# Values of the cross attention from 512 weight columns per matmul, in a three-mixer decoder trunk on one core

## The chip, the core and the metric

The program runs on one core of a Trainium2 chip. It is launched once, and the metric is the device time of that launch in microseconds (us). Names of engines are those of the profile: PE multiplies matrices (PEld are its weight loads), ACT, DVE and POOL work element by element, SP starts most transfers from device memory. A program is written as one stream; a scheduler orders the instructions of each engine and puts semaphores between them, and each engine then works its own list in that order.

## What is computed

Four layers on 256 tokens of width 1024, float32. A layer is a token mixer (Mamba-2, HGRN2, gated DeltaNet, then Mamba-2 again), a cross attention into 256 memory tokens, and a gated feed-forward block. The part that the change touches is the product of the normalised memory with the second half of `wkv`, once per layer:

```python
def memory_cross_attention(h, mem_n, wq, wkv, wo):
    q = (h @ wq).reshape(bsz, seq, X_HEADS, X_HEAD_DIM)
    k, v = jnp.split(mem_n @ wkv, 2, axis=-1)
    ...
    s = jnp.einsum('blhd,bmhd->bhlm', q, k).astype(jnp.float32) * X_HEAD_DIM ** -0.5
    p = jax.nn.softmax(s, axis=-1).astype(h.dtype)
    o = jnp.einsum('bhlm,bmhd->blhd', p, v).reshape(bsz, seq, D_MODEL)
    return o @ wo
```

Here `mem_n` is 256 x 1024 and each half of `wkv` 1024 x 1024.

## The kernel before

Every product with weights is made of three matmuls. A float32 number is split into a rounded part H and a rest L, both in the type fp32r, and `mm3` (lines 166 to 170) adds H·H, H·L and L·H into one bank of PSUM. The memory is split once per layer into `mH` and `mL` (`mem_split`), while the feed-forward block of the layer before is running. The weights are split as they arrive: `prep` (lines 150 to 164) fetches a piece of 128 x 1024 numbers (512 KB) through SP's queue into the tile `raw`, rounds it on ACT (`wH`, line 160) and subtracts on DVE (`wL`, line 161). There are four buffers of `raw`, three of `wH` and three of `wL`, shared by all products with weights in the program. `prep` runs under a raised priority (300), so the scheduler places its instructions as far ahead of the matmuls as the buffers allow.

`mem_kv` (lines 344 to 383) makes keys and values of a layer ahead of its mixer. Its first half is the keys, its second half the values. For each of four blocks of 256 output columns it takes two pieces (`kh`, 512 rows of the weights each) and issues 48 matmuls in groups of three:

```python
                            if half == 0:
                                c = slice(k * T + cb * P, k * T + (cb + 1) * P)
                                mm3(d, H[:, c], L[:, c], mH[:, kt, :], mL[:, kt, :], first, last)
                            else:
                                c = slice(k * T, (k + 1) * T)
                                t = slice(cb * P, (cb + 1) * P)
                                mm3(d, mH[:, kt, t], mL[:, kt, t], H[:, c], L[:, c], first, last)
```

For the values the memory is the operand that is loaded into the array (128 columns of it), and 256 columns of a weight piece stream past it. So the values of one layer are 4 x 2 x 2 x 4 x 3 = 192 matmuls of 256 columns, into four banks named `kvps`. ACT then moves a bank to the tile `Vt`, scaled (line 353). DVE moves the keys to `KTt` (line 349).

What stands around this in a layer from the second on: the last products of the feed-forward block (`f_down`, in `out_proj`, banks `acc`), whose last four pieces are half as large; then DVE adds the banks to the residual `xT` (line 283), ACT squares it (`nsq`, line 200), POOL sums the squares (`ns`, lines 203 and 206), and a matmul `ps_nrm` (line 210) in the middle of the keys sums over partitions. From its result the normalised input of the mixer is made (`nh`, `hH`, `hL`) while PE is at the keys. After the values PE goes on with the mixer's first product, in the bank `fps` (HGRN2), `baps` (gated DeltaNet) or `dtps` (Mamba-2). Small latency-bound parts of the program are woven in between by a counter of estimated PE time (`weave.tick`). The first layer makes the sums of squares of the memory along with its keys (`stats` is not None there), at a time when the first transfers of the program are running.

Pools opened by `phase` take SBUF one behind the other and are given back when they close; a tile in a new pool waits for the instructions that used the same addresses before.

Of the kernel before, what the change touches and what calls it, by code (L numbers as in the profile page):

```python
# [8 lines left out]
F32 = mybir.dt.float32  # L9
F32R = mybir.dt.float32r  # L10
U32 = mybir.dt.uint32
AF = mybir.ActivationFunctionType
ALU = mybir.AluOpType
# [3 lines left out]
P = 128  # L17
D = 1024
T = 256
KT = 8  # L20
# [3 lines left out]
PRIO = 400  # L24
# [62 lines left out]
def tile_trunk(ctx: ExitStack, tc: tile.TileContext, io: dict, out: bass.AP, layers=range(DEPTH), parts="mxf", final=True):  # L87
    nc = tc.nc
    ACT, DVE, POOL, PE = nc.scalar, nc.vector, nc.gpsimd, nc.tensor
    weave = Weave()  # L90
# [7 lines left out]
    PRIO, EVAC = [300,150]  # L98
# [9 lines left out]
    def phase(name, bufs=1):  # L108
        return tc.tile_pool(name=name, bufs=bufs, reuse_waits="tile")
# [4 lines left out]
    def bank(name):  # L114
        return ps_acc.tile([P, 512], F32, tag="acc", name=name)
# [8 lines left out]
    def f32(ap):  # L124
        return ap.bitcast(F32)
# [10 lines left out]
    Vt = cst.tile([P, 2, D], F32, name="Vt")  # L136
# [10 lines left out]
    rsmc = cst.tile([P, 2], F32, name="rsmc")  # L147
# [4 lines left out]
    def prep(src, n=1024, step=1024):  # L152
        with tc.high_priority(offset=PRIO):
            raw = wp.tile([P, 1024], F32, tag="raw", name="raw", bufs=WB[0])
            H = wp.tile([P, 1024], F32R, tag="wH", name="wH", bufs=WB[1])
            L = wp.tile([P, 1024], F32R, tag="wL", name="wL", bufs=WB[2])
            for o in range(0, n, step):
                c = slice(o, min(n, o + step))
                nc.sync.dma_start(out=raw[:, c], in_=src[:, c])
                ACT.copy(H[:, c], raw[:, c])  # L160
                DVE.tensor_tensor(out=L[:, c], in0=raw[:, c], in1=f32(H[:, c]), op=ALU.subtract)  # L161
                if len(between) > 1:
                    between[-1](between.pop(0))
        return H, L

    def mm3(dst, aH, aL, bH, bL, start, stop):

        PE.matmul(dst, aH, bH, start=start, stop=False, skip_group_check=True)  # L168
        PE.matmul(dst, aH, bL, start=False, stop=False, skip_group_check=True)  # L169
        PE.matmul(dst, aL, bH, start=False, stop=stop, skip_group_check=True)  # L170
# [58 lines left out]
    def proj(srcs, ps):  # L229

        for i, s in enumerate(srcs):
            H, L = prep(s)
            for kt in range(KT):
                c = slice(kt * P, (kt + 1) * P)
                mm3(ps[:, i * T:(i + 1) * T], H[:, c], L[:, c], hH[:, kt, :], hL[:, kt, :],
                    i == 0 and kt == 0, kt == KT - 1)
                if kt % 2:
                    weave.tick(654)

    def proj_tok(srcs, ps):  # L240

        for kh, s in enumerate(srcs):
            H, L = prep(s)
            for mt in range(2):
                for k in range(4):
                    kt = 4 * kh + k
                    t = slice(mt * P, (mt + 1) * P)
                    c = slice(k * T, (k + 1) * T)
                    mm3(ps[:, mt * T:(mt + 1) * T], hH[:, kt, t], hL[:, kt, t], H[:, c], L[:, c],
                        kt == 0 and mt == 0, kt == KT - 1)  # L250
                    if k % 2:
                        weave.tick(654)

    def out_proj(wsrc, nk, a, gens=None, gname=None, layer=0, last=False):
# [5 lines left out]
        for g in range(ng):  # L260
# [10 lines left out]
            for b in range(4):  # L271
                H, L = prep(wsrc[g, b], n * T)
                for cb in range(2):
                    for k in range(n):
                        kt = 4 * g + k
                        c = slice(k * T + cb * P, k * T + (cb + 1) * P)
                        mm3(accs[b][:, cb * T:(cb + 1) * T], H[:, c], L[:, c], aH[k], aL[k],
                            kt == 0 and cb == 0, kt == nk - 1)
                        if k % 2:
                            weave.tick(654)  # L280
                if g == ng - 1:
                    xs = flat(xT[:, 2 * b:2 * b + 2, :])
                    DVE.tensor_tensor(out=xs, in0=xs, in1=accs[b], op=ALU.add)
                    if gname is not None:
                        for kt in (2 * b, 2 * b + 1):
                            split_gain(xT[:, kt, :], pcol(gname, layer * 8 + kt), hH[:, kt, :], hL[:, kt, :])
                    st.add(xs)
                    if last:
                        for kt in (2 * b, 2 * b + 1):
                            fg = pcol("final", kt)  # L290
                            if b < 3:
                                POOL.tensor_scalar(out=KTt[:, kt, :], in0=xT[:, kt, :], scalar1=fg, scalar2=None, op0=ALU.mult)
                            else:
                                ACT.activation(out=KTt[:, kt, :], in_=xT[:, kt, :], func=AF.Copy, scale=fg)
# [42 lines left out]
    def mem_rs(stats):  # L337
        stats.rs(rsm)
        tp = mx("rsmt")
        for mt in range(2):  # L340
            PE.transpose(tp[:, mt * P:(mt + 1) * P], rsm[:, mt * P:(mt + 1) * P], ident)
        ACT.copy(rsmc, tp[:, :T].rearrange("p (a b) -> p a b", a=2)[:, :, 0])

    def mem_kv(layer, mH, mL, stats=None):
        todo = []

        def evac(half, b, ps):
            if half == 0:
                DVE.tensor_tensor(out=KTt[:, 2 * b:2 * b + 2, :], in0=ps.rearrange("p (a b) -> p a b", a=2),
                                  in1=rsm.unsqueeze(1).to_broadcast([P, 2, T]), op=ALU.mult)  # L350
            else:
                for mt in range(2):
                    ACT.activation(out=Vt[:, mt, b * T:(b + 1) * T], in_=ps[:, mt * T:(mt + 1) * T], func=AF.Copy,
                                   scale=rsmc[:, mt:mt + 1])

        for half in range(2):
            for b in range(4):
                ps = bank("kvps")
                for kh in range(2):
                    H, L = prep(io["xa_kv"][layer, half, b, kh], step=512 if stats is not None else 1024)  # L360
                    for cb in range(2):
                        for k in range(4):
                            kt = 4 * kh + k
                            d = ps[:, cb * T:(cb + 1) * T]
                            first, last = kt == 0 and cb == 0, kt == KT - 1
# [7 lines that stand above are left out]
                            if k % 2:  # L373
                                weave.tick(654)
                todo.append((half, b, ps))
                if stats is not None:
                    if b == 0:
                        continue
                    mem_rs(stats)
                    stats = None  # L380
                for u in todo:
                    evac(*u)
                todo = []


    def attention(layer, st):
# [773 lines left out]
    for i, l in enumerate(layers):  # L1160
        nrm = weave.push(late(NL[0], norm_h(st, "ln_mix", l) if i else x_stats())) if mix else None
        if m is not None:
            mem_kv(l, *m)
            kv.close()
        if mix:
            weave.finish([nrm])
            st = (mamba, hgrn, gdn)[l % 3](l, l // 3, "ln_xattn" if "x" in parts else "ln_ffn" if "f" in parts else None)
        else:
            for kt in range(KT):
                g = "ln_xattn" if "x" in parts else "ln_ffn"  # L1170
                split_gain(xT[:, kt, :], pcol(g, l * 8 + kt), hH[:, kt, :], hL[:, kt, :])
        if "x" in parts:
            st = attention(l, st)
        m, hook = mem_start(i + 1)
        if "f" in parts:
            st = ffn(l, st, hook, final and i == len(layers) - 1)
        elif hook is not None:
            hook()
# [5 lines left out]
    for b in range(4):  # L1184
        o = Vt.rearrange("p a (b t) -> p (a b) t", t=T)[:, 2 * b:2 * b + 2, :]
        (POOL if b == 3 else DVE).tensor_tensor(out=o, in0=KTt[:, 2 * b:2 * b + 2, :],
                                                in1=rs.unsqueeze(1).to_broadcast([P, 2, T]), op=ALU.mult)
# [123 lines left out]
```

## Time and profile before

| | us |
|---|---|
| median of 3 runs | 2069.55 |
| the three runs | 2066.68, 2069.55, 2073.19 |
| the profiled execution | 2072.47 |
| its span, from its first to its last instruction | 2070.7 |
| PE busy in the span | 2025.5 (98%) |
| DVE busy | 1590.6 (77%) |
| ACT busy | 1282.5 (62%) |
| POOL busy | 344.5 (17%) |

The profile shows one execution. A matmul's busy time overlaps that of the next one, since matmuls are pipelined: what a matmul costs in a stream is read from the distance between starts, not from its own length. The profile's span and the time of the execution differ by 1.8 us that lie around the program.

### The profile page before, as it was taken

To read this page: it belongs to the slowest core of one execution; us is meant where nothing else is said; L and a number is where in the kernel's file an instruction comes from. 1 tells how busy PE (TensorE), PEld (TensorE's weight loads), DVE (VectorE), ACT (ScalarE), POOL (GpSimd) and SP (SyncE) were. 2 spreads that over 40 slices of the span, in tenths; PEclk is the share of its full clock that TensorE was granted. 3 is DMA by queue.
4 is the path that set the end of the run, shared out by engine and by line. 5 is a ranking of instruction groups with operands and counts; after the bars stand their busy time and mean duration, and the time that the engine had idled before them with its cause. 6 is when DMAs were issued, how large, how long until landed. Compare 5 with 4: busy or idle time off the path is not lost.

```text
span 2070.7 us, 42162 instructions
## 1 busy us (share of the span) xinstructions
PE 2025.5 (98%) x17084; PEld 1971.5 (95%) x17084; DVE 1590.6 (77%) x2423; ACT 1282.5 (62%) x1874; POOL 344.5 (17%) x468
## 2 busy tenths in 40 slices
PE   8999999999999999999999999999999999999997
PEld 8999999999999899999988889999999999999997
DVE  6899787875688777866786775778757999778765
ACT  6677666654565566555676875666545777666553
POOL 2032211000132110001064451110000223201001
PEclk9999999999999999999999999999999999999999
DMA  7554555655654446666543333456656444545663
GB/s 239 163 155 152 162 154 162 206 188 170 206 157 140 149 137 195 203 195 192 186 130 126 114 113 115 139 163 211 195 179 196 151 154 150 174 133 183 186 189 115
DMA packets 110372, 343.10 MB, mean 166 GB/s; under 512 B 15456, under 2 KB 25312, under 8 KB 110176
## 3 DMA queue, kind: packets, MB, share of 16 engines
q1 hardware_dynamic: 106176, 333.42, 52.0%
q10 hardware_dynamic: 3744, 6.71, 1.0%
q8 instruction: 134, 2.20, 0.4%
q0 software_dynamic: 256, 0.26, 0.1%
q14 instruction: 62, 0.51, 0.1%
HBM read 336.42 MB, written 3.93 MB: 164 GB/s over the span
## 4 chain that ended last, share of the span: by engine, by line
PE 79%; DVE 6%; issue 5%; ACT 4%; DMA 3%; POOL 2%; ACTq 0%; SPq 0%; DVEq 0%; POOLq 0%
PE acc L168 7%; PE ffps L170 7%; PE acc L169 7%; PE ffps L169 7%; PE ffps L168 7%; PE acc L170 7%; PE mps L168 4%; PE mps L169 4%; PE mps L170 4%; DVE wL L161 2%; PE kvps L170 2%; PE kvps L168 2%; PE kvps L169 2%; PE qps L170 2%; PE qps L168 2%
## 5 line engine op out<-in xcount | busy, mean ns | idle before, releaser
L161 DVE TENSOR_TENSOR wL<-raw,wH 128x1024 fp32r<-128x1024 f32 (+2 forms) x639 | 776.1, 1216 | 318.9 <-ACT wH L160 316.6
L160 ACT CAST wH<-raw 128x1024 fp32r<-128x1024 f32 (+2 forms) x639 | 658.4, 1031 | 510.6 <-PE ffps L169 156.4
L168 PE MATMUL acc<-aH,wH 128*128 128x256 f32 x1408 | 396.4, 282 | 0.6 <-ACT aH L173 0.6
L170 PE MATMUL ffps<-hH,wL 128*128 128x256 f32 x1408 | 392.6, 279 | 1.8 <-DVE wL L161 1.7
L168 PE MATMUL ffps<-hH,wH 128*128 128x256 f32 x1408 | 392.0, 279 | 2.5 <-ACT hH L183 2.5
L170 PE MATMUL acc<-aH,wL 128*128 128x256 f32 x1408 | 393.0, 279 | 0.0
L169 PE MATMUL acc<-aL,wH 128*128 128x256 f32 x1408 | 392.4, 279 | 0.1
L169 PE MATMUL ffps<-hL,wH 128*128 128x256 f32 x1408 | 392.1, 279 | 0.2
L168 PEld LDWEIGHTS ffps<-hH,wH 128*128 128x128 f32 x1408 | 265.5, 189 | 3.4 <-ACT hH L183 3.3
L168 PEld LDWEIGHTS acc<-aH,wH 128*128 128x128 f32 x1408 | 265.2, 189 | 3.5 <-issue 1.3
L170 PEld LDWEIGHTS ffps<-hH,wL 128*128 128x128 f32 x1408 | 264.4, 188 | 4.1 <-DVE wL L161 3.7
L169 PEld LDWEIGHTS acc<-aL,wH 128*128 128x128 f32 x1408 | 265.6, 189 | 1.5 <-issue 0.5
L169 PEld LDWEIGHTS ffps<-hL,wH 128*128 128x128 f32 x1408 | 265.1, 188 | 1.1 <-DVE hL L184 0.6
L170 PEld LDWEIGHTS acc<-aH,wL 128*128 128x128 f32 x1408 | 264.6, 188 | 0.4 <-DVE wL L161 0.2
L168 PE MATMUL mps<-hH,wH 128*128 128x256 f32 x768 | 219.8, 286 | 0.0
L170 PE MATMUL mps<-hH,wL 128*128 128x256 f32 x768 | 215.0, 280 | 0.0
L169 PE MATMUL mps<-hL,wH 128*128 128x256 f32 x768 | 214.9, 280 | 0.0
L203 POOL TENSOR_TENSOR ns<-nsq 128x256 f32<-128x256 f32 x13 | 10.5, 811 | 856.5 <-ACT nsq L200 856.5
L168 PEld LDWEIGHTS mps<-hH,wH 128*128 128x128 f32 x768 | 145.1, 189 | 2.7 <-issue 2.4
L170 PEld LDWEIGHTS mps<-hH,wL 128*128 128x128 f32 x768 | 145.4, 189 | 0.1
L169 PEld LDWEIGHTS mps<-hL,wH 128*128 128x128 f32 x768 | 144.5, 188 | 0.3
L170 PE MATMUL gps<-hH,wL 128*128 128x256 f32 x448 | 127.2, 284 | 0.9 <-DVE wL L161 0.9
(397 smaller groups left out, 4489.9 us busy)
## 6 DMA issues: line engine op xcount, KB each, us to landing
raw<-f_up SPq DMA_DIRECT2D x176, 512.0 KB, 3.6
raw<-m_in SPq DMA_DIRECT2D x96, 512.0 KB, 3.5
raw<-f_down SPq DMA_DIRECT2D x80, 512.0 KB, 3.5
raw<-xa_kv SPq DMA_DIRECT2D x60, 512.0 KB, 4.2
raw<-g_in SPq DMA_DIRECT2D x48, 512.0 KB, 3.9
raw<-m_out SPq DMA_DIRECT2D x32, 512.0 KB, 3.5
raw<-xa_q SPq DMA_DIRECT2D x32, 512.0 KB, 3.5
raw<-xa_o SPq DMA_DIRECT2D x32, 512.0 KB, 3.5
```

The costliest lines, as they stand in the source:

```text
L160: ACT.copy(H[:, c], raw[:, c])
L161: DVE.tensor_tensor(out=L[:, c], in0=raw[:, c], in1=f32(H[:, c]), op=ALU.subtract)
L168: PE.matmul(dst, aH, bH, start=start, stop=False, skip_group_check=True)
L169: PE.matmul(dst, aH, bL, start=False, stop=False, skip_group_check=True)
L170: PE.matmul(dst, aL, bH, start=False, stop=stop, skip_group_check=True)
L203: self.eng.tensor_tensor(out=self.sum, in0=sq[:, :T], in1=sq[:, T:], op=ALU.add)
```

## The change

From the second layer on the values are made by a new function, `wide_values`. Two blocks of 256 columns are taken together: `prep2` fetches a pair of pieces, rounds and subtracts each as `prep` does, but into tiles of their own (`raw2`, `wH2`, `wL2`) in a pool that exists for the values alone. Each matmul streams 512 columns, 256 from each piece of the pair, into a whole bank `vps`. A layer's values are 96 matmuls of 512 columns and four instructions on ACT that move 512 columns each to `Vt`. The raised priority of `prep2` is a third of `prep`'s, and there are two buffers of each of its tiles, for four pairs. The first layer keeps the old form. Keys are unchanged.

```diff
+    def prep2(srcs, pool):
+
+        with tc.high_priority(offset=PRIO // 3):
+            raw = pool.tile([P, 2, 1024], F32, tag="raw2", name="raw2")
+            H = pool.tile([P, 2, 1024], F32R, tag="wH2", name="wH2")
+            L = pool.tile([P, 2, 1024], F32R, tag="wL2", name="wL2")
+            for i in range(2):
+                nc.sync.dma_start(out=raw[:, i, :], in_=srcs[i])
+                ACT.copy(H[:, i, :], raw[:, i, :])
+                DVE.tensor_tensor(out=L[:, i, :], in0=raw[:, i, :], in1=f32(H[:, i, :]), op=ALU.subtract)
         return H, L
...
+    def wide_values(layer, mH, mL):
+
+        with phase(f"vw{layer}", 2) as vw:
+            vw.tile([P, 48], F32, name="vpad", bufs=1)
+            for b in range(2):
+                pv = [bank("vps") for _ in range(2)]
+                for kh in range(2):
+                    H, L = prep2([io["xa_kv"][layer, 1, 2 * b + i, kh] for i in range(2)], vw)
+                    for mt in range(2):
+                        t = slice(mt * P, (mt + 1) * P)
+                        for k in range(4):
+                            kt = 4 * kh + k
+                            c = slice(k * T, (k + 1) * T)
+                            mm3(pv[mt], mH[:, kt, t], mL[:, kt, t], H[:, :, c], L[:, :, c], kt == 0, kt == KT - 1)
+                            weave.tick(600)
+                for mt in range(2):
+                    ACT.activation(out=Vt[:, mt, b * 512:(b + 1) * 512], in_=pv[mt], func=AF.Copy,
+                                   scale=rsmc[:, mt:mt + 1])
+
     def mem_kv(layer, mH, mL, stats=None):
         todo = []
+        wide = stats is None
...
-        for half in range(2):
+        for half in range(1 if wide else 2):
...
+        if wide:
+            wide_values(layer, mH, mL)
```

The change also moves the splitting of the pairs in the lists of the engines. On DVE, at the end of the first layer's feed-forward block, the list before reads as follows (`wL_6537` and `wL_6560` belong to the last two half pieces of `f_down`, `wL_6585` to the first piece of the keys):

```order
L161 TENSOR_TENSOR wL_6537<-raw_6535,wH_6536 128x512
L283 TENSOR_TENSOR xT_79<-xT_79,acc0_5841 128x512
L161 TENSOR_TENSOR wL_6560<-raw_6558,wH_6559 128x512
L283 TENSOR_TENSOR xT_79<-xT_79,acc1_5842 128x512
L161 TENSOR_TENSOR wL_6585<-raw_6583,wH_6584 128x1024
L283 TENSOR_TENSOR xT_79<-xT_79,acc2_5843 128x512
L161 TENSOR_TENSOR wL_6615<-raw_6613,wH_6614 128x1024
```

With the change DVE's list at the same place is this; the first half of pair 2 stands first, its second half comes between the last half piece of `f_down` and the first piece of the keys:

```order
L175 TENSOR_TENSOR wL2_6908<-raw2_6906,wH2_6907 128x1024
L161 TENSOR_TENSOR wL_6514<-raw_6512,wH_6513 128x512
L161 TENSOR_TENSOR wL_6537<-raw_6535,wH_6536 128x512
L295 TENSOR_TENSOR xT_79<-xT_79,acc0_5841 128x512
L161 TENSOR_TENSOR wL_6560<-raw_6558,wH_6559 128x512
L175 TENSOR_TENSOR wL2_6908<-raw2_6906,wH2_6907 128x1024
L161 TENSOR_TENSOR wL_6585<-raw_6583,wH_6584 128x1024
L295 TENSOR_TENSOR xT_79<-xT_79,acc1_5842 128x512
```

Pairs 1 and 2 are thus split ahead of the keys, and the addition to the residual from the second bank has moved behind the first piece of the keys. The same holds in the two later layers.

On ACT, at the values of the second layer, the list before is:

```order
L160 CAST wH_6962<-raw_6961 128x1024
L160 CAST wH_6995<-raw_6994 128x1024
L353 ACTIVATE Vt_81<-kvps_6867,rsmc_94 128x256 x2
L160 CAST wH_7025<-raw_7024 128x1024
L160 CAST wH_7058<-raw_7057 128x1024
L353 ACTIVATE Vt_81<-kvps_6930,rsmc_94 128x256 x2
```

With the change ACT's list there is this (`wH_7137` is the third piece of the mixer that follows; `wH2_6944` is pair 3, `wH2_6977` pair 4):

```order
L160 CAST wH_7137<-raw_7136 128x1024
L174 CAST wH2_6944<-raw2_6943 128x1024 x2
L372 ACTIVATE Vt_81<-vps_6871,rsmc_94 128x512
L174 CAST wH2_6977<-raw2_6976 128x1024 x2
L372 ACTIVATE Vt_81<-vps_6872,rsmc_94 128x512
L372 ACTIVATE Vt_81<-vps_6941,rsmc_94 128x512
L372 ACTIVATE Vt_81<-vps_6942,rsmc_94 128x512
L680 DMA hc_7017<-cm 128x388
```

Three pieces of the mixer now stand ahead of pairs 3 and 4, which are the only weights split during the values.

## Rows read from the trace of the kernel before

**Rows 1.** The page: busy time, share of the span and instructions, and the chain's shares.
```profile
PE 2025.5 (98%) x17084; PEld 1971.5 (95%) x17084; DVE 1590.6 (77%) x2423; ACT 1282.5 (62%) x1874; POOL 344.5 (17%) x468
...
PE 79%; DVE 6%; issue 5%; ACT 4%; DMA 3%; POOL 2%; ACTq 0%; SPq 0%; DVEq 0%; POOLq 0%
```

**Rows 2.** Windows: two f_down stages, then the three values stages that change.
```profile
core 0: us, PE busy (x) PEld busy (x) DVE busy (x) ACT busy (x) POOL busy (x), PEclk, DMA share, GB/s
...
892.94:952.78 59.84, 59.84 (x530) 59.84 (x529) 34.10 (x38) 30.45 (x36) 1.59 (x2) 1.00 0.61 180
458.42:520.61 62.19, 62.19 (x531) 62.19 (x529) 34.23 (x37) 30.51 (x36) 1.72 (x2) 1.00 0.56 172
543.66:566.27 22.61, 22.61 (x195) 22.61 (x194) 11.04 (x12) 10.61 (x14) 0.00 (x0) 1.00 0.65 194
975.00:996.76 21.76, 21.76 (x194) 21.76 (x193) 10.78 (x12) 10.09 (x14) 0.00 (x0) 1.00 0.63 193
1572.32:1594.08 21.76, 21.76 (x194) 21.76 (x193) 10.85 (x13) 9.99 (x14) 0.00 (x0) 1.00 0.60 191
```

**Rows 3.** Groups by line on PE in the values stage from 975.00 (one of three).
```profile
L168 PE MATMUL kvps<-wH,mH 128*128 128x256 f32 x64 | 17.7, 276 | 0.0
```

**Rows 4.** Timeline of PE: end of values, layer two; first mixer product, layer four.
```profile
566.15 0.28 PE L170 MATMUL kvps<-wH,mL 128*128 128x256 f32 x1
566.27 0.28 PE L168 MATMUL fps<-hH,wH 128*128 128x256 f32 x1
...
1594.08 0.28 PE L168 MATMUL dtps<-hH,wH 128*32 128x256 f32 x1
...
1596.83 0.28 PE L168 MATMUL mps<-hH,wH 128*128 128x256 f32 x1
```

**Rows 5.** Instructions of two tiles: weight loads, ns min/median/max, first and last start.
```profile
L168 PEld LDWEIGHTS kvps<-wH,mH x256: 187/187/188, 33.7 to 1593.6; 128*128 128x128 f32 x128
...
L168 PEld LDWEIGHTS dtps<-hH,wH x16: 107/108/108, 56.5 to 1596.4; 128*32 128x32 f32 x16
```

**Rows 6.** Timeline of PE around one wait in the first layer's f_up.
```profile
392.80 0.28 PE L168 MATMUL ffps<-hH,wH 128*128 128x256 f32 x1
...
395.52 0.28 PE L168 MATMUL ffps<-hH,wH 128*128 128x256 f32 x1
...
396.37 0.39 PE L170 MATMUL ffps<-hH,wL 128*128 128x256 f32 x1 [0.45 <-DVE wL L161]
396.59 0.28 PE L168 MATMUL ffps<-hH,wH 128*128 128x256 f32 x1
...
400.12 0.28 PE L168 MATMUL ffps<-hH,wH 128*128 128x256 f32 x1
```

**Rows 7.** Timeline of ACT and DVE in the values stage from 975.00.
```profile
980.64 1.06 ACT L160 CAST wH<-raw 128x1024 fp32r<-128x1024 f32 x1 [1.62 <-PE kvps L170]
981.60 0.82 ACT L353 ACTIVATE Vt<-kvps,rsmc 128x256 f32<-128x256 f32 x2
...
981.73 1.23 DVE L161 TENSOR_TENSOR wL<-raw,wH 128x1024 fp32r<-128x1024 f32 x1 [1.45 <-ACT wH L160]
```

**Rows 8.** The page, DMA issues: KB each, median us to landing.
```profile
raw<-xa_kv SPq DMA_DIRECT2D x60, 512.0 KB, 4.2
```

**Rows 9.** Timeline of ACT, DVE, PE where f_down gives way to the keys, layer three.
```profile
950.22 1.04 ACT L160 CAST wH<-raw 128x1024 fp32r<-128x1024 f32 x1
...
950.26 0.69 DVE L283 TENSOR_TENSOR xT<-xT,acc 128x512 f32<-128x512 f32 x1
951.30 1.23 DVE L161 TENSOR_TENSOR wL<-raw,wH 128x1024 fp32r<-128x1024 f32 x1 [0.35 <-ACT wH L160]
...
952.78 0.28 PE L168 MATMUL kvps<-mH,wH 128*128 128x256 f32 x1
```

**Rows 10.** Timeline of POOL and PE: sums of squares and the matmul that takes them.
```profile
951.93 7.91 POOL L206 TENSOR_TENSOR ns<-ns,nsq 128x256 f32<-128x256 f32 x6 [0.79 <-ACT nsq L200]
...
963.66 0.38 PE L210 MATMUL ps_nrm<-ns,ones 128*128 128x256 f32 x1
```

More of the change, by code (lines that the diff above doesn't have):

```diff
@@ L163, in prep @@
                     between[-1](between.pop(0))
+        return H, L
+    def prep2(srcs, pool):
[7 more added lines that the diff above has]
+                DVE.tensor_tensor(out=L[:, i, :], in0=raw[:, i, :], in1=f32(H[:, i, :]), op=ALU.subtract)
         return H, L
```

## The prediction, made before the changed kernel was run

> **What bounds the kernel now.** I read the page first: PE is busy 98% of the span and holds 79% of the chain that ended last, while DVE stands at 77% and ACT at 62% [rows 1]. So time is won where PE needs fewer nanoseconds, and lost where PE is made to wait. Second, the windows over the three values stages that change: 22.61, 21.76 and 21.76 us, in each of which PE is busy from end to end, at a granted clock of 1.00, with ACT busy about 10 us and DVE about 11 [rows 2]. The groups by line show 64 matmuls of 256 columns for each of the three products [rows 3], 192 in all. The last of them and the first of the mixer start 0.12 us apart, like any two neighbours [rows 4]: there is no wait at that end which a faster stage could run into or remove.
>
> Third, the pace. 21.76 us over 192 is 113.3 ns from start to start, 22.61 over 192 is 117.8 ns. The two f_down stages, 528 equal matmuls each (22 x 4 x 2 x 3), give 59.84/528 = 113.3 and 62.19/528 = 117.8 [rows 2]. So PE has two paces, 4% apart, at the same granted clock, and each holds for whole stages. In the first layer's f_up I see one turn into the other: 24 matmuls in 2.72 us (113.3) up to 395.52, a wait for a subtraction at 396.37, then 30 in 3.53 us (117.7) [rows 6]. I don't know what sets the pace; a wait of PE can change it.
>
> At the granted level of 2.4 GHz, 256 columns at one per tick are 106.7 ns. What is left, 6.6 ns at the quick pace and 11.1 at the slow one, is paid per matmul.
>
> **What the change saves on PE.** Each layer's values become 96 matmuls of 512 columns. Is the remainder a cost per matmul, or is it the weight load? A load of 128 columns lasts 187 ns, one of 32 columns 108 [rows 5], yet the 24 matmuls behind loads of 32 columns take 2.75 us, 114.6 ns each [rows 4]. A shorter load doesn't quicken the stream, so I take the remainder as a fixed cost per matmul. Then a matmul of 512 columns costs 213.3 + 6.6 = 219.9 ns where the pace is quick, and 213.3 + 11.1 = 224.4 where it is slow. Two stages: 192 x 219.9 = 42.22 us; one: 96 x 224.4 = 21.54; together 63.76 against 66.13 now, **2.4 us less**.
>
> The trace has no such matmul of this type, so both ends: with no fixed cost at all, 288 x 213.3 = 61.44, 4.7 us less; if the remainder grows with the columns, nothing is saved; if in addition all three stages ran at the slow pace, 576 x 117.8 = 67.85, 1.7 us more. I keep 2.4, which treats the remainder as the loads of 32 columns suggest, and both ends for the range.
>
> A rule speaks against this gain. The Trainium skill, page "TensorE: Matmul & The Clock Gate", section "Wait — 56ns, not 53.3ns?", gives a warm matmul N/2.4 + about 2.5 ns. By it 256 columns would take 109.2 ns, and the 288 matmuls removed would save 288 x 2.5 = 0.7 us instead of 2.4. This trace doesn't agree with it at 256 columns: 113.3 and 117.8.
>
> **Splitting the pairs.** The number of pieces fetched, rounded and subtracted is unchanged, so nothing is won or lost in work; what moves is when. Pairs 3 and 4 are the only ones split during the values, each after PE frees the buffer of the pair two before. From the rows of such a stage: ACT starts at once when PE frees a buffer (1.62 us idle up to then), a rounding takes 1.06 us, the subtraction starts 1.09 us behind its start and takes 1.23 [rows 7]. Two pieces: 1.09 + 1.23 + 1.23 = 3.55 us from freed to ready. PE meanwhile works on the other pair, 24 x 0.22 = 5.28 us. That leaves 1.7 us: cost nothing, covered by that other pair; without the cover each of six waits would cost up to 3.55. In ACT's list only a move to `Vt` stands between. The four moves of 512 columns to `Vt` replace eight of 256 that take 0.82 us in twos [rows 7]; at twice the length each they are no longer in sum, and nothing needs them before the attention, a whole mixer later. The mixer gains little: three of its pieces are ready at its start, but PE didn't wait there before.
>
> **The seam from f_down to the keys.** Pairs 1 and 2 are split here, four extra roundings (1.05 each) and four subtractions (1.23 each). While f_down runs on whole pieces there is room: DVE is busy 34 of 60 us [rows 2]. The tight point is the first piece of the keys. Before, its subtraction ran from 951.30 to 952.53, after DVE had idled 0.35 us for the rounding that began at 950.22; PE's keys start at 952.78 and want the rest L with the third matmul, at 953.01 [rows 9]. Now the subtraction of a half pair (1.23) stands where the addition to the residual (0.69, at 950.26) stood. DVE would do it from about 950.4 to 951.6 and the keys' piece from 951.6 to 952.9: some 0.1 us to spare. Bounds: nothing, or the whole 1.23 us per layer. I take 0.1 for each of three layers, since half pieces leave small gaps on both engines, **0.3 us more**.
>
> Behind that point on DVE stands the addition to the residual from the second bank, about 2.5 us later than now, and behind it the squares on ACT and the sums on POOL. They end at 951.93 + 7.91 = 959.84 and PE takes them at 963.66 [rows 10]: 3.8 us of cover for a delay of 2.5. Nothing, but this is what is late next.
>
> Transfers: in SP's list the first one of pair 1 waits for the last split of the gated activations, with two half pieces of f_down behind it; those themselves wait for later subtractions, so they lose nothing. A transfer lands 4.2 us after its issue [rows 8], and the DMA engines are busy 56 to 61% in these stages [rows 2]. Nothing. Later transfers of keys and mixer keep their own buffers.
>
> **Sum.** 2.4 less and 0.3 more: 2.1 us less. Against the profiled execution, 2072.47, that is 2070.4; this execution lay 2.9 us above the median of the runs, 2069.55, so the median to expect is **2067.4 us**. A measurement of this kernel can tell about 0.3% (6.2 us) from no change, so most cases end inside it.
>
> **Rivals.**
> - *No gain per column.* The remainder is paid in step with the columns (say, by reading the moving operand). For it: a load a third as wide changes nothing, so the load isn't it; no row excludes it. Time: 2069.6 to 2071.3. Chance 0.12.
> - *The pace changes elsewhere.* New small waits at the seam, or other arrival times, put a feed-forward block on the other pace. f_up has twice the matmuls of f_down, so a block is some 180 us and 4% of it 7.1 us. For it: the same code ran in 62.19 us in one layer and 59.84 in another [rows 2], and a short wait stood at one switch [rows 6]. Against: the change leaves those blocks alone, and the runs shown differ by 6.5 us already. One block to the quick pace: 2060.3; one to the slow: 2074.5. Chance 0.13: 0.07 down, 0.06 up, and of these 0.03 with more than one block, beyond 0.3%.
> - *The pairs come late* (slower). Pairs 3 and 4 have 1.7 us to spare. If something delays them beyond, PE stands in each of three layers twice. To end over 6.2 us above now it must first eat the 2.1 us gained: 8.3/6 = 1.4 us per wait, that is 6.7 us to get a pair ready instead of 3.55. Time: 2075.8. For it: subtractions lengthen where POOL is at work; against: POOL is idle during the values [rows 2] and ACT's list holds nothing else there. Chance 0.04.
> - *The pace belongs to the matmul, not to its columns*: then half the matmuls would go for nothing, 192 x 113.3 + 96 x 117.8 = 33.1 us, 2036.5. Against it: 113.3 ns is 6% above what the columns alone need. Chance 0.02. A rule of the Trainium skill points this way: the same page, section "Back-to-back issue gap", reports a sustained 131 ns for 512 columns, by which the three stages would shrink by 66.1 - 288 x 0.131 = 28.4 us; no row here shows a stream beyond one column per tick.
>
> That the change doesn't do what it says is excluded: the lists show 288 matmuls fewer, and 288 of 512 columns in the three layers.
>
> **How the numbers follow.** The forecast has 0.69. Faster by over 0.3%: 0.07 for a block turned quick, 0.02 for the last rival, 0.05 for the forecast's good end met by the scatter of the runs: 0.14. Slower: 0.04 for late pairs, 0.03 for slow blocks, 0.01 for scatter: 0.08. The rest, 0.78, is no change that can be told. The range reaches to one block turned either way, 2060.3 to 2074.5, which holds the bounds of the unknown costs too.
>
> **What would show it.** In the changed profile the values stages should last about 21.5, 21.1 and 21.1 us, starts 220 to 224 ns apart, and PE without a gap over 0.1 us inside them. A gap on PE at the second pair of either block would be the late pairs; a gap at the first or second matmul group of the keys the seam; a gap before `ps_nrm` the late sums. Equal stages of 21.8 to 22.6 us would mean no gain per column. The prediction is wrong if the median leaves the range, or if it falls in the range by other stages than these.

## The result, and the profile after

| | before, us | after, us |
|---|---|---|
| median of 5 runs each, taken in turn | 2069.55 | 2079.71 |
| lowest and highest | 2065.75, 2073.19 | 2076.62, 2086.52 |
| the profiled execution | 2072.47 | 2086.52 |
| its span | 2070.7 | 2084.7 |

The ratio is 1.0054, 95% interval 1.0028 to 1.0079: the change makes the kernel slower, by 5.8 to 16.3 us. I had forecast 2067.4 with a range up to 2074.5. A second set of ten runs of the same kernel gave 2083.08 against 2068.93 (ratio 1.0079, interval 1.0048 to 1.0111).

The page of the changed kernel has 288 matmuls fewer than [rows 1], as the change intends, yet PE's busy time didn't shrink and DMA's share of the chain of waits rose from 3 to 4%:

```profile
PE 2033.0 (98%) x16796; PEld 1964.7 (94%) x16796; DVE 1588.8 (76%) x2423; ACT 1279.3 (61%) x1862; POOL 343.9 (16%) x468
...
PE 77%; DVE 7%; issue 6%; ACT 4%; DMA 4%; POOL 2%; SPq 0%; ACTq 0%; DVEq 0%; POOLq 0%
```

The windows of the changed kernel over two f_down stages and the three values stages, in the columns of [rows 2]:

```profile
core 0: us, PE busy (x) PEld busy (x) DVE busy (x) ACT busy (x) POOL busy (x), PEclk, DMA share, GB/s
455.67:516.70 61.03, 60.43 (x531) 60.03 (x529) 36.65 (x39) 32.66 (x38) 0.74 (x1) 1.00 0.65 215
890.24:955.98 65.74, 63.20 (x531) 62.70 (x530) 39.43 (x42) 33.80 (x39) 0.73 (x1) 0.95 0.65 211
541.25:563.65 22.40, 22.40 (x98) 17.96 (x97) 6.92 (x8) 7.01 (x8) 0.00 (x0) 1.00 0.15 48
979.03:1001.43 22.40, 22.40 (x99) 17.88 (x97) 6.83 (x7) 7.02 (x8) 0.01 (x1) 1.00 0.14 48
1585.96:1608.35 22.39, 22.39 (x99) 17.97 (x98) 7.09 (x9) 7.09 (x9) 0.00 (x0) 1.00 0.15 48
```

Two things stand here. The values stages last 22.40 us each, 67.19 together, where [rows 2] have 66.13 and I expected 63.76: they cost 1.1 us instead of saving 2.4. And f_down, whose code isn't touched, took 65.74 us in layer three, 5.9 more than in [rows 2], with PE busy for 63.20 of it at a mean granted clock of 0.95. Much of the rest went there. PE's timeline in that stage, at the last half pieces of `f_down`:

```profile
945.88 0.28 PE L182 MATMUL acc<-aH,wL 128*128 128x256 f32 x1
947.96 0.39 PE L180 MATMUL acc<-aH,wH 128*128 128x256 f32 x1 [1.80 <-ACT wH L160]
948.18 0.39 PE L181 MATMUL acc<-aL,wH 128*128 128x256 f32 x1
949.30 0.58 PE L182 MATMUL acc<-aH,wL 128*128 128x256 f32 x1 [0.73 <-DVE wL L161]
949.68 0.42 PE L180 MATMUL acc<-aH,wH 128*128 128x256 f32 x1
949.90 0.42 PE L181 MATMUL acc<-aL,wH 128*128 128x256 f32 x1
```

The start at 947.96 comes 2.08 us after the one before, the start at 949.30 1.12 us after its neighbour: PE waited for a rounding, then for the subtraction of the same half piece. From 949.90 on the starts lie 213 to 218 ns apart, 25 of them, where they were 113. Windows of the same place show the granted clock at 0.50, its lower level of 1.2 GHz. The mean of 0.55 from 948 to 950 says that it fell near 948.2, behind the first wait and ahead of the second:

```profile
946.00:948.00 2.00, 0.20 (x3) 0.04 (x1) 1.80 (x2) 1.80 (x4) 0.00 (x0) 1.00 0.46 188
948.00:950.00 2.00, 1.27 (x5) 0.96 (x6) 2.00 (x4) 0.99 (x2) 0.00 (x0) 0.55 0.66 233
950.00:952.00 2.00, 2.00 (x11) 2.00 (x11) 1.40 (x3) 1.86 (x4) 0.38 (x1) 0.50 0.71 238
952.00:954.00 2.00, 2.00 (x12) 2.00 (x11) 2.00 (x2) 0.72 (x1) 0.35 (x1) 0.50 0.87 320
```

What made the rounding late is on ACT, and what made ACT late in SP's list. First the issues (SP's queue: start, length of the issue), then ACT's timeline. L173 and L174 are the transfers and the roundings of pairs 1 and 2, though the trace prints `raw` and `wH` for `raw2` and `wH2`:

```profile
930.74 3.05 SPq L159 DMA_DIRECT2D raw<-f_down  x2
934.65 0.33 SPq L173 DMA_DIRECT2D raw<-xa_kv  x1
936.18 0.33 SPq L159 DMA_DIRECT2D raw<-f_down  x1
936.55 0.90 SPq L173 DMA_DIRECT2D raw<-xa_kv  x2
938.90 0.33 SPq L159 DMA_DIRECT2D raw<-f_down  x1
```

```profile
938.92 1.05 ACT L174 CAST wH<-raw 128x1024 fp32r<-128x1024 f32 x1 [1.30 <-DVE wL L161]
939.88 0.61 ACT L160 CAST wH<-raw 128x512 fp32r<-128x512 f32 x1
945.09 1.05 ACT L174 CAST wH<-raw 128x1024 fp32r<-128x1024 f32 x1 [4.60 <-DMA raw<-xa_kv]
946.35 1.04 ACT L174 CAST wH<-raw 128x1024 fp32r<-128x1024 f32 x1 [0.20 <-DMA raw<-xa_kv]
947.30 1.13 ACT L160 CAST wH<-raw 128x512 fp32r<-128x512 f32 x2
```

ACT did nothing for 4.60 us. It stood at the rounding of the second half of pair 1, whose transfer, issued at 936.55, had not landed: 8.5 us from issue to the rounding's start, where [rows 8] have a median of 4.2. Behind it in ACT's list stood the first half of pair 2 (946.35) and then the second and third half pieces of `f_down` (947.30, x2), whose transfers had been issued before its own, the later at 936.18. PE needed the first of them at 946.0. ACT works its list in the written order, so they waited for a weight that PE would want 33 us later. Before, ACT took the same two half pieces as soon as PE had freed a buffer, and PE had no wait in this stage [rows 2]:

```profile
944.71 0.62 ACT L160 CAST wH<-raw 128x512 fp32r<-128x512 f32 x1 [2.10 <-PE acc L169]
947.43 0.62 ACT L160 CAST wH<-raw 128x512 fp32r<-128x512 f32 x1 [2.10 <-PE acc L169]
```

The same picture stands in layers two and four, without the fall of the clock: PE's starts are 0.66, 0.50 and 1.47 us apart in layer two and 0.79, 0.38 and 1.47 in layer four, the last of the three each time at the third matmul of the keys. That one in layer two, on PE, with the subtraction it waits for in DVE's timeline:

```profile
518.27 0.39 PE L182 MATMUL kvps<-mH,wL 128*128 128x256 f32 x1 [1.19 <-DVE wL L161]
```

```profile
514.69 0.69 DVE L161 TENSOR_TENSOR wL<-raw,wH 128x512 fp32r<-128x512 f32 x1 [1.35 <-ACT wH L160]
515.30 1.78 DVE L175 TENSOR_TENSOR wL<-raw,wH 128x1024 fp32r<-128x1024 f32 x1
517.01 1.21 DVE L161 TENSOR_TENSOR wL<-raw,wH 128x1024 fp32r<-128x1024 f32 x1
```

Here DVE waits for the rounding of the last half piece, then does the second half of pair 2 (1.78 us, longer than the usual 1.23), then the first piece of the keys. POOL works on the first sum of squares from 515.27 to 516.00, within those 1.78 us; in the profile of before none of the 508 subtractions of this size without POOL at work beside it took over 1.23 us.

The delays add up as follows. Of each start that comes over 0.15 us after its neighbour, the part beyond 0.116 us is counted, from the end of f_down to the end of the keys, less the 0.29 us that the same count gives there before: 3.0 us in layer two, 5.8 in layer three (some 2.5 of them at the lower clock), 2.6 in layer four, 11.4 in all. With the 1.1 us of the values that is 12.5 of the 14.0 us between the two profiled spans. The second profile of the same kernel has 3.2, 1.8 and 2.9, 7.9 us, at the same places and with no fall of the clock.

### The profile page after: what moved, and what is told of

It reads as the page before. It is cut to its first block, busy times and chain, and to the rows that moved or that the text cites. A ratio compares the mean times of both kernels' runs of the same rounds, so it can differ in the third digit from the quotient of the medians.

```text
span 2084.7 us, 41539 instructions
## 1 busy us (share of the span) xinstructions
PE 2033.0 (98%) x16796; PEld 1964.7 (94%) x16796; DVE 1588.8 (76%) x2423; ACT 1279.3 (61%) x1862; POOL 343.9 (16%) x468
## 4 chain that ended last, share of the span: by engine, by line
PE 77%; DVE 7%; issue 6%; ACT 4%; DMA 4%; POOL 2%; SPq 0%; ACTq 0%; DVEq 0%; POOLq 0%
PE ffps L182 7%; PE ffps L180 7%; PE ffps L181 7%; PE acc L180 6%; PE acc L181 6%; PE acc L182 6%; PE mps L180 4%; PE mps L181 4%; PE mps L182 4%; DVE wL L161 3%; PE qps L182 2%; PE qps L181 2%; PE qps L180 2%; ACT wH L160 1%; PE kvps L182 1%
## 5 line engine op out<-in xcount | busy, mean ns | idle before, releaser
L161 DVE TENSOR_TENSOR wL<-raw,wH 128x1024 fp32r<-128x1024 f32 (+2 forms) x615 | 744.4, 1212 | 283.2 <-ACT wH L160 280.3
L160 ACT CAST wH<-raw 128x1024 fp32r<-128x1024 f32 (+2 forms) x615 | 632.5, 1030 | 465.3 <-PE ffps L181 158.6
```

## The experiments

Three theories were tested. **S**: the loss is made at the seam, where pairs 1 and 2 are fetched and split. **W**: it is made by the wide matmuls. **P**: it is chance, PE's two paces falling otherwise.

**Narrow matmuls from the same pairs.** Everything is fetched and split as in the change, but each matmul of 512 columns is made as two of 256.

```diff
-                            mm3(pv[mt], mH[:, kt, t], mL[:, kt, t], H[:, :, c], L[:, :, c], kt == 0, kt == KT - 1)
+                            for i in range(2):
+                                mm3(pv[mt][:, i * T:(i + 1) * T], mH[:, kt, t], mL[:, kt, t], H[:, i, c], L[:, i, c],
+                                    kt == 0 and i == 0, kt == KT - 1)
```

> Pairs fetched and split as in the change, but each matmul of 512 columns is made as two of 256 again. Theory S (the loss of some 10 us is made at the end of f_down and the start of the keys, where pairs 1 and 2 are fetched and rounded): the waits of PE there stay, the values stages take about 21.8 us each (192 x 113.3 ns) instead of 22.4, and the time stays at 2078 to 2080. Rival W (the wide matmuls themselves lose the time): back to about 2069.6. Rival P (chance of PE's two paces): no order, anything from 2065 to 2085.

Measured: 2082.94, ratio to before 1.0061 (1.0036 to 1.0086). The loss stays without a single wide matmul, and so do PE's waits: 2.5, 2.5 and 2.4 us by the count above, at the half pieces of `f_down` and the third matmul of the keys, as here in layer three:

```profile
952.30 0.39 PE L182 MATMUL acc<-aH,wL 128*128 128x256 f32 x1 [0.85 <-DVE wL L161]
...
957.66 0.38 PE L182 MATMUL kvps<-mH,wL 128*128 128x256 f32 x1 [1.00 <-DVE wL L161]
```

W falls as the main cause.

**Wide matmuls without pairs.** The weights are laid out so that a piece is 256 rows by 512 columns. They come one by one through the old `prep` and its ring, in the order of before, and a matmul streams 512 columns that lie together.

```diff
-                    H, L = prep2([io["xa_kv"][layer, 1, 2 * b + i, kh] for i in range(2)], vw)
+                H, L = prep(io["xa_kv"][layer, 1, n // 2, n % 2])
...
-                            c = slice(k * T, (k + 1) * T)
-                            mm3(pv[mt], mH[:, kt, t], mL[:, kt, t], H[:, :, c], L[:, :, c], kt == 0, kt == KT - 1)
+                        c = slice(k * 512, (k + 1) * 512)
+                        mm3(pv[mt], mH[:, kt, t], mL[:, kt, t], H[:, c], L[:, c], kt == 0, kt == KT - 1)
```

> Matmuls of 512 columns without pairs: the weights of the values are laid out so that one piece holds 256 rows of 512 columns, fetched and split by the old function through the old buffers in the old order. S: no new waits at the end of f_down; values stages of 22.4 us as in the change (233.3 ns per matmul), 2069.6 + 1.1 = 2070.7. If the 233 ns come from reading two separate runs of 256 columns, 220 ns here, stages of 21.1 and 2067.3. W: 2079.7, as the change. P: no order.

Measured: 2070.0, ratio 0.9995 (0.9961 to 1.0029). The loss is gone, with no gap on PE at the seam. The values take 21.97 to 21.99 us, neither the 22.4 nor the 21.1 that were expected. The windows of f_down and of the values in layer three:

```profile
895.22:957.40 62.18, 62.18 (x530) 62.18 (x529) 34.22 (x37) 30.46 (x36) 1.72 (x2) 1.00 0.55 175
980.04:1002.02 21.98, 21.98 (x98) 17.99 (x97) 10.79 (x12) 9.85 (x11) 0.00 (x1) 1.00 0.57 189
```

So 288 matmuls fewer, with nothing else disturbed, gain nothing that can be told either: the three stages sum to 65.94 against 66.13.

**Roundings late, transfers early.** The change, with the roundings of pairs 1 and 2 put behind those of the third to sixth piece of the keys in ACT's list. `behind` only orders the list; the transfers still start at the end of f_down. `prep2` has the full raised priority of `prep` here, as in the next run and the sixth.

```diff
+                h = ACT.copy(H[:, i, :], raw[:, i, :])
+                if after is not None:
+                    behind([h], [after[i]])
-                ACT.copy(H[:, i, :], raw[:, i, :])
...
+            keys = rounded[-8:]
...
-                    H, L = prep2([io["xa_kv"][layer, 1, 2 * b + i, kh] for i in range(2)], vw)
+                    H, L = prep2([io["xa_kv"][layer, 1, 2 * b + i, kh] for i in range(2)], vw,
+                                 keys[2 + 2 * kh:] if b == 0 else None)
```

> The change, with the roundings of pairs 1 and 2 put behind the roundings of keys' pieces 3 to 6 in ACT's list, at the full raised priority; their transfers stay at the end of f_down. S as a matter of ACT's order (a rounding that waits for its transfer holds up the half pieces of f_down behind it): waits at the seam gone, 2070.7. S as a matter of bandwidth (six transfers of 512 KB crowd the half pieces): the waits stay, near 2079. W: 2079.7.

Measured: 2072.36, ratio 1.0021 (0.999 to 1.0052); no gap of PE at the seam in any layer. The windows of f_down, keys and values in layer three:

```profile
888.63:948.47 59.84, 59.84 (x530) 59.84 (x529) 34.11 (x38) 30.51 (x36) 1.59 (x2) 1.00 0.64 214
948.47:970.69 22.22, 22.22 (x196) 22.17 (x195) 21.77 (x30) 15.42 (x23) 8.36 (x6) 1.00 0.84 289
970.69:993.09 22.40, 22.40 (x99) 18.01 (x97) 8.79 (x11) 7.71 (x10) 0.01 (x1) 1.00 0.20 72
```

PE is busy for the whole of f_down again, at a DMA share of 0.64 that is no lower than the change's 0.65, and the median landing of these pieces is 5.3 us, against the change's 5.4. The slowest transfer of the crowd at the end of f_down in this layer took 7.5 us, against 9.2 in the change. Late landing of this size alone thus costs nothing here; it costs when something else stands behind it on ACT. The keys have no slack left on DVE: 21.77 of 22.22 us busy.

**Roundings and transfers late.** As the last, and the transfers too stand behind those roundings: `behind([d, h], [after[i]] * 2)`, with `d` the transfer.

> As the run before, with the transfers of pairs 1 and 2 put behind those roundings as well. S in either form: no waits at the seam, 2070.7 with values stages of 22.4 us, unless the pairs then come late for the values: each us of that shows as a gap of PE at the start of the values. W: 2079.7.

Measured: 2071.04, ratio 1.0 (0.9976 to 1.0025), no gaps at the seam. Holding back the transfers as well adds nothing that can be told.

**Three forms of the same stage.** Here all values come through the ring as in the second experiment, but layer two streams 512 columns that lie together, layer three the same as two runs of 256, which is how the change reads them, and layer four uses two matmuls of 256. The layout of each layer's weights follows.

```diff
+                        if layer == 1:
+                            mm3(pv[mt], mH[:, kt, t], mL[:, kt, t], H[:, c], L[:, c], kt == 0, kt == KT - 1)
+                        elif layer == 2:
+                            Hs, Ls = [x.rearrange("p (i k t) -> p i k t", i=2, k=2)[:, :, k, :] for x in (H, L)]
+                            mm3(pv[mt], mH[:, kt, t], mL[:, kt, t], Hs, Ls, kt == 0, kt == KT - 1)
+                        else:
+                            for i in range(2):
+                                c = slice(k * 512 + i * T, k * 512 + (i + 1) * T)
+                                mm3(pv[mt][:, i * T:(i + 1) * T], mH[:, kt, t], mL[:, kt, t], H[:, c], L[:, c],
+                                    kt == 0 and i == 0, kt == KT - 1)
-                        mm3(pv[mt], mH[:, kt, t], mL[:, kt, t], H[:, c], L[:, c], kt == 0, kt == KT - 1)
```

> Values of the three later layers in three forms, all from pieces of 256 rows x 512 columns fetched and split through the old ring: layer two 512 columns that lie together, layer three the same 512 columns as two runs of 256 (as the change reads them), layer four two matmuls of 256. Everything else alike. If the remainder beyond one column per tick depends on the number of runs: about 229, 233 and 2 x 113 to 118 ns from start to start, stages of 22.0, 22.4 and 21.8 to 22.6 us. If the 233 ns of the change came from its own tiles, or from what else goes on during its stages (ACT and DVE splitting pairs, more transfers), layers two and three are alike, both near 229. If it is a fixed cost per matmul as I predicted, layers two and three are near 220 to 224. No gap on PE at the seam in any layer, since the pieces come through the ring.

The windows over the three stages, in this order (a single run, 2078.28 us, which says nothing on the time):

```profile
539.73:561.70 21.97, 21.97 (x98) 18.05 (x97) 11.45 (x12) 10.38 (x11) 0.00 (x0) 1.00 0.65 202
979.15:1001.55 22.40, 22.40 (x99) 18.11 (x98) 10.37 (x12) 9.83 (x11) 0.01 (x1) 1.00 0.55 179
1584.25:1606.86 22.61, 22.61 (x195) 22.60 (x194) 10.45 (x13) 9.71 (x11) 0.00 (x0) 1.00 0.56 177
```

21.97/96 = 228.9 ns, 22.40/96 = 233.3, 22.61/192 = 117.8. With ACT, DVE and the transfers alike, two runs cost 4.4 ns more than one, and a matmul of 512 columns costs about what two of 256 do (226.7 at the quick pace, 235.6 at the slow one). The 22.40 us of the change are a property of the operand, not of what went on beside it.

**Roundings moved a little.** The change, with the roundings of pairs 1 and 2 only behind that of the last half piece of `f_down`: in the third experiment's edit, `[rounded[-9]] * 2` takes the place of `keys[2 + 2 * kh:]`. They now stand among the first pieces of the keys.

> The change, with the four roundings of pairs 1 and 2 moved in ACT's list by only three to eight places: right behind the rounding of the last half piece of f_down, in between the first pieces of the keys. Their transfers start as early as in the change. Theory H (head of the line: ACT stands at a rounding whose transfer hasn't landed, and the f_down half pieces behind it, landed long before, wait with it): by then the transfers have landed, so no gap of PE over 0.3 us in f_down, at most one small one at the keys, and a time of before within 0.3%, 2065 to 2075. Theory L (load: four more roundings and four more subtractions, 4.2 and 4.9 us, are too much around the start of the keys wherever they stand): gaps of 1 us or more stay, now at the second and third piece of the keys, some 3 to 6 us in all three layers, and a time of 2073 to 2080. If both hold a part, gaps only at the keys and no half clock in layer three.

Measured: 2092.93, ratio 1.0129 (1.0077 to 1.018, four runs), the slowest of all. Theory H is right about f_down: 59.84 us in layer two and 62.19 in the others, PE's two plain paces, with no gap, and at the third matmul of the keys the starts are only 0.27 to 0.38 us apart. But the keys last 30.77, 29.79 and 29.46 us. L is thus right that the load is too much there, but neither theory had the place. It is in the middle of the keys. DVE's timeline of layer two (the edit shifts the lines: L162 and L178 are the subtractions of `prep` and `prep2`, L298 the addition to the residual):

```profile
515.84 3.61 DVE L162 TENSOR_TENSOR wL<-raw,wH 128x1024 fp32r<-128x1024 f32 x3
519.37 2.90 DVE L178 TENSOR_TENSOR wL<-raw,wH 128x1024 fp32r<-128x1024 f32 x2
522.19 1.21 DVE L162 TENSOR_TENSOR wL<-raw,wH 128x1024 fp32r<-128x1024 f32 x1
523.33 1.76 DVE L178 TENSOR_TENSOR wL<-raw,wH 128x1024 fp32r<-128x1024 f32 x1
525.01 1.75 DVE L162 TENSOR_TENSOR wL<-raw,wH 128x1024 fp32r<-128x1024 f32 x1
526.68 1.27 DVE L298 TENSOR_TENSOR xT<-xT,acc 128x512 f32<-128x512 f32 x2
```

And PE's, where `ps_nrm` (now L225) needs the sums that POOL makes from those additions:

```profile
527.77 0.28 PE L185 MATMUL kvps<-mH,wL 128*128 128x256 f32 x1
533.20 1.22 PE L225 MATMUL ps_nrm<-ns,ones 128*128 128x256 f32 x2 [5.15 <-POOL ns L221]
533.86 0.78 PE L183 MATMUL kvps<-mH,wH 128*128 128x256 f32 x1
```

DVE worked without a pause, yet the last two additions to the residual stood behind eight subtractions and started at 526.68. The squares and the sums followed, and PE waited 5.15 us, after which its starts lay 214 ns apart, 21 of them.

**The change once more**, for a second profile and ten more times.

> The changed kernel once more, on the chip of the other runs of this job, for a second profile and more times. If the seam is the cause, its gaps stand at the same three places of each later layer (two f_down half pieces, the third group of the keys), worth some 2 to 6 us a layer whatever pace PE has, and the time is 0.3 to 0.8% above before: 2076 to 2086. If the loss was one of PE's paces by chance, the gaps are there or not and the time comes down to that of before within 0.2%.

Measured: 2083.08, ratio 1.0079 (1.0048 to 1.0111). The gaps stand at the same places: 0.70, 1.18 and 1.34 us between starts in layer two, 0.58 and 1.28 in layer three, 0.37, 1.12 and 1.43 in layer four. P falls as the cause: the loss repeats, and its gaps with it, while PE spent 848 us in stretches at the slow pace here, 893 in the first profile of the change and 875 before.

No version beat the kernel before. Those that mend the seam, by the ring or by late roundings, only come back to its time.

## Why the prediction was wrong, point by point

I forecast 2.1 us less, and the medians show 10.2 us more. Two terms of the sum failed: the values cost 1.1 us instead of saving 2.4, and the seam cost 8 to 11 us instead of 0.3.

**What bounds the kernel**: right. PE is the bound, and in the changed values it is busy from end to end.

**The gain on PE**: wrong. The step that failed is "I take the remainder as a fixed cost per matmul", inferred from weight loads of 32 columns that don't quicken the stream [rows 4, 5]. Those rows exclude the load; they don't say that the remainder stays when the columns double. Measured, the remainder beyond one column per tick is 228.9 - 213.3 = 15.6 ns for 512 columns in one run and 20.0 for two runs, against 6.7 or 11.1 for 256. It roughly doubles with the columns, and the second run adds to it. My rival "no gain per column" was the right one as to size: for it I gave the values 66.13 to 67.85 us, and they took 67.19. What in the stream makes the remainder grow isn't shown. The Trainium skill, page "TensorE: Matmul & The Clock Gate", section "Wait — 56ns, not 53.3ns?", gives 215.7 ns for 512 columns at the higher clock. The runs here, in fp32r and with a load for each matmul, show 228.9 and 233.3. That page spoke for less gain than I took, which came out, but not for its reason: its 2.5 ns too are a fixed cost per matmul, and the remainder here grows with the columns. For the lower clock the same section of the Trainium skill gives N/1.2 GHz, by which 256 columns would take an estimated 213.3 ns. The 213 to 218 ns behind the waits in layer three agree.

**Splitting pairs 3 and 4 at no cost**: right. PE has no gap inside any values stage, in any of the runs.

**The seam**: wrong, and by far the larger error. I took 0.3 us with 1.23 per layer as the upper end; it cost 2.6 to 5.8 per layer in one profile and 1.8 to 3.2 in the other. Two of my sentences failed. "While f_down runs on whole pieces there is room" is true of the sum, DVE 34 of 60 us busy [rows 2], and in layer three ACT idled 4.60 us at a stretch. But room is no protection when the list is in order and its head waits for a transfer. "A transfer lands 4.2 us after its issue ... Nothing" took a median from a kernel in which the pieces of the keys and values come singly. Here three transfers of 512 KB and two half pieces were issued within 4.3 us, and one took 8.5. What I left out was to lay SP's list beside ACT's: in SP's, the transfer of pair 1's second half comes behind those of the second and third half pieces; in ACT's, its rounding stands ahead of theirs.

The tight point that I did price, the first piece of the keys behind a pair's subtraction on DVE, is there: its wait was put at 0.1, at most 1.23 us, and the starts show 1.47 - 0.12 = 1.35 us in layers two and four. I had worked it out from an ACT that is in time; ACT was late, and the subtraction took 1.78 us instead of 1.23. In the second profile this one wait makes 3.7 of the 7.9 us; most of the rest stands at the half pieces of `f_down`, of which I had written "so they lose nothing".

**What is late next**: the place was right, the delay too small. I put the sums at 3.8 us of cover against a delay of 2.5. Counted from the start of the keys, they end 5.7, 2.1 and 3.9 us later than before. PE still finds them ready in layers three and four, with 2.1 and 1.8 us to spare, but waits 0.19 us for them in layer two, where 4.4 us were to spare before:

```profile
529.40 0.70 PE L222 MATMUL ps_nrm<-ns,ones 128*128 128x256 f32 x2 [0.19 <-POOL ns L218]
```

In the sixth experiment POOL's sums of that layer end another 3.8 us later (533.15 against 529.35), and this wait became the largest of all.

**The rivals**: I had a slower case with the right kind of mechanism, pairs that come late, at the wrong place. I looked for it at pairs 3 and 4, where PE needs them soon, and not at pairs 1 and 2, which PE needs late but which stand ahead of something that it needs at once. The change of pace elsewhere, my other wide rival, isn't what happened: 893 and 848 us at the slow pace, against 875 before. That the pace belongs to the matmul, not to its columns, is out by 228.9 and 233.3 ns.

**Lead**: the lower priority of `prep2` does nothing for the seam. With none, or with that of `prep`, the lists of ACT and SP are the same there; only pair 4 moves, by one place, and no run has either alone. What seems to decide the place is when the pool's addresses come free: in layer three the first transfer of pair 1 waits 0.8 us for a split of the gated activations (`aL`). No run tests that.

## What to carry to other kernels

When a change moves a load with its processing ahead, lay the issue list beside the list of the engine that takes the data, and for each entry ask what is behind it and how soon that is wanted; a busy share of 50% on that engine says little. Work that is wanted late belongs behind work that is wanted soon, and how far behind is to be read from the next chain on the same engines: here four to six places cured one wait and made a larger one, nine to twelve cured both. And a cost per instruction inferred at one size should be held as one end of a range until a row has it at the other size.

## What the runs showed of the hardware that was not expected

- The remainders of a matmul beyond one column per tick stand in even steps: 6.7 ns (256 columns, quick pace), 11.1 (256, slow pace), 15.6 (512 in one run), 20.0 (512 in two runs), each 4.4 ns above the last. Each of the two forms of 512 columns has one pace in all profiles, whatever the pace around it. At the granted clock of 0.50 the remainder was gone: 213 ns for 256 columns, in the change and in the sixth experiment.
- PE's two paces can move a single run by more than the change does. The third experiment's profile had 544 us in stretches at the slow pace and a span of 2059.4, the fourth's, with the same instructions on PE, 1212 us and 2085.9: 26.5 us for 668 us, 4.0%, the distance between the paces. What sets the pace stays open; no run was aimed at it.
- In one profile of the change the granted clock fell to 0.50 right behind a wait of 2.08 us from start to start, with a second of 1.12 us on top, and 25 starts followed at that level. In the other, waits of 0.70 and 1.18 us in the same code were not followed by a fall. In the sixth experiment a wait of 5.4 us in each layer was, with 21, 10 and 10 starts at the lower level.
